# Three row tiles of the next block under way instead of two, in a streaming encoder layer on one core

## The chip, the cores and the metric

The kernel runs as one program on 1 core of one Trainium2 chip. The metric is the device time of one execution in microseconds (us); three executions of the kernel before are known, and their median is the time before. A profile of one further execution goes with them.

## The reference, cut to what matters

The reference is one layer of a streaming encoder over 2048 prompt rows and 64 sample rows of width 1024, in float32. What matters here is its first step, which every row goes through before the input projection:

```python
def rms_norm(x, g):
    xf = x.astype(jnp.float32)
    y = xf * lax.rsqrt(jnp.mean(xf * xf, axis=-1, keepdims=True) + NORM_EPS)
    return (y * g.astype(jnp.float32)).astype(x.dtype)

h = rms_norm(x, p['norm1_g']) * (1 + sc1) + sh1
z = h @ p['w_in']
```

`z` is then cut into a convolution branch, q, k and v of an attention over the row's own chunk of 64 and the 8 chunks before it, and two gates. Both branches are projected, gated and merged, projected again and added to the input; a feed-forward part with a second norm follows.

## The kernel before, in words

**Blocks and stages.** The 2112 rows (64 sample rows first) are worked in four blocks (`PBLOCKS`, line 35: 576 rows, then 512 three times) and then, from about 1200 us of the span, in three other blocks for merge, output projection and feed-forward. For each of the four blocks the stages run in the order of line 553: q, a quarter of the convolution's input, k, another quarter, v, the last two quarters, and the gates ("g"). Every product is made of three passes (`mm3`, line 700) of operands that are split in a high and a low part.

**The normed rows.** All products of a block read `hh` and `hl` (lines 1606, 1607): the normed, scaled and transposed rows of that block, high and low part, eight slices of 128 channels by up to 576 columns. There is one pair of them. So the rows of the next block are written into it while the gates of this block, its last readers, are still at work, columns first to last as they come free.

**One row tile.** `norm_tile` (line 1166) is a generator that prepares one tile of 128 rows of the next block, step by step; a `yield` ends a step and says when the next is due. Its steps are:

1. The row tile `x_t` is loaded (`load_ahead`, line 1160) into one of three buffers (tag "x", line 1164). Three tiles are loaded when the generators are made known; the fourth is loaded when the first tile has gone through its second group of transposes and left its buffer (line 1183).
2. The square (line 1147): ScalarE squares two halves of 512 with a running sum, into two scratch tiles `junk` of the ring "t" (seven buffers, line 773, which also holds the gates' results until their DMA has stored them, and others); VectorE adds the two sums and forms the mean; GpSimd raises it to the power -1/2 (`r`, line 740).
3. The scale (line 1175): VectorE multiplies the 128x1024 tile by `r`, in place.
4. Twice, for a group `g` of four slices: TensorE transposes four 128x128 pieces into a PSUM bank `pt` (line 1181), VectorE applies the norm's weight and shift into `h` (line 1187), the generator waits until the gates have left the columns it will write (line 1189), ScalarE writes `hh` (line 1191) and VectorE `hl` (line 1193).

**What orders the work.** The kernel is written as one stream of instructions around the matmuls. After a set of passes `stream.spend` (line 207) may make a tick, one per 500 ns of counted TensorE time, and at a tick each lane (`Lane`, line 108) may take one step of one of its generators. The lanes are the norm lane, q/k rows, attention heads, the convolution's tail and the convolution's taps (line 1604). The norm lane takes the first of its first `NORM_W` = 2 generators whose next step is due (line 146). So while the tiles with number 0 and 1 of the next block wait for columns, the tiles 2 and 3 are not begun; tile 2 is begun when tile 0 is done.

The norm lane gets the four generators of the next block when gate 11 of 16 is done (lines 1645 to 1650). The gates' last two pairs are worked in two halves of the columns, and `free["columns"]` is set after each half (line 1373). At stage q of the next block, `qkv` (line 1194) goes through the four tiles in order; for each it first steps the tile's generator to its end if it is not there yet (line 1210), and then writes the 24 matmuls of the product (line 1213). So the products of q meet the four tiles just after they were made. This happens three times in the kernel: at the ends of blocks 0, 1 and 2.

The framework that builds the program may put the instructions of one engine in another order than they were written in; each engine then works through its own list in that order. SyncE ("SP") issues nearly all DMAs, in one list too.

Of the kernel before, what the change touches and what calls it, by code (L numbers as in the profile page):

```python
# [16 lines left out]
P = 128  # L17
# [36 lines left out]
SIDE_G = 10  # L54
SPLIT_G = 2
NORM_G = 11
NORM_W = 2
SCORE_ROOM = {"dve": 2500}
TURN_NS = 600.0
POOL_BEHIND = 3000.0  # L60
# [4 lines left out]
def token_tiles(lo, hi):  # L65
    head = [(0, SMP)] if lo == 0 else []
    return head + [(t, P) for t in range(max(lo, SMP), hi, P)]
# [10 lines left out]
def tile_chunks(lo, hi):  # L78

    tiles = token_tiles(lo, hi)  # L80
    t, n = tiles[(len(tiles) + 1) // 2 - 1]
    return [(lo, t + n), (t + n, hi)]
# [529 lines left out]
def streaming_layer(ctx: ExitStack, tc: tile.TileContext, I, O):  # L612
# [87 lines left out]
    def mm3(ps, lh, ll, rh, rl, first, last, **kw):  # L700
        pe.matmul(ps, lh, rh, start=first, stop=False, **kw)
        pe.matmul(ps, lh, rl, start=False, stop=False, **kw)
        pe.matmul(ps, ll, rh, start=False, stop=last, **kw)
        stream.spend()
# [67 lines left out]
    def temp(name, shape=(P, 512)):  # L772
        return wk.tile(list(shape), F32, tag="t", name=name, bufs=NT)
# [312 lines left out]
    def v_rows(ps, n, t):  # L1086
        out = state_row(vs_p, vn_s, t, n)
        store_v(ps, n, kcol(t))
        if out is not None:
            v32 = temp("v32")  # L1090
            act.activation(v32[:n], ps[:n], AF.Copy)
            stream.at(stream.when("act"), lambda: nc.sync.dma_start(out, v32[:n]))
# [17 lines left out]
    def state_row(prompt, sample, t, n):  # L1110
        if t < SMP:
            return sample[:n]
        t -= SMP + SEQ - QB
        return prompt[t : t + n] if t >= 0 else None

    def kcol(t):
        return t + CACHE
# [16 lines left out]
    def load_mixed(c0, c1, i):  # L1134

        src = [[quarter("cin", i) for _ in range(2)] for _ in range(2)]
        for j, a in enumerate((c_d, o_d)):
            for l in range(2):
                nc.sync.dma_start(src[l][j][:, :, : c1 - c0].bitcast(F32), a[l, :, :, c0:c1].rearrange("c p t -> p c t"))
        return src  # L1140
# [6 lines left out]
    def square(x_t, n, junk=None):  # L1147
        ssq = wk.tile([P, 2], F32, tag="ssq", name="ssq", bufs=3)
        if junk is not None:
            act.activation(junk[:n], x_t[:n], AF.Square, accum_out=ssq[:n, 0:1])  # L1150
            return rsqrt_mean(wk, ssq[:n, 0:1], n, 1, D)
        for j in range(2):
            act.activation(temp("junk")[:n], x_t[:n, 512 * j : 512 * j + 512], AF.Square, accum_out=ssq[:n, j : j + 1])
        stream.after("dve", "act")
        dve.tensor_tensor(ssq[:n, 0:1], ssq[:n, 0:1], ssq[:n, 1:2], ALU.add)
        return rsqrt_mean(wk, ssq[:n, 0:1], n, 1, D)
# [3 lines left out]
    def load_ahead():  # L1160

        if to_load:
            t = to_load.pop(0)
            ahead_x[t] = load_x(t, P, wa, "x", 3), stream.load["pe"] + X_LAG

    def norm_tile(lo, t, free):

        c = slice(t - lo, t - lo + P)
        while t not in ahead_x:
            load_ahead()  # L1170
        x_t, landed = ahead_x.pop(t)
        yield landed
        r = square(x_t, P)
        yield stream.when("pool")
        dve.tensor_scalar(x_t, x_t, r, None, ALU.mult)
        yield stream.when("dve") + PE_LAG
        for g in range(2):
            pt = ps_g.tile([P, 4, P], F32, tag="gp", name="pt")
            h = temp("h32", (P, 4, P))
            for k in range(4):  # L1180
                pe.transpose(pt[:, k], x_t[:, (4 * g + k) * P : (4 * g + k + 1) * P], ident)
            if g:
                stream.at(stream.when("pe"), load_ahead, True)
            stream.after("dve", "pe")
            for k in range(4):
                kk = 4 * g + k
                dve.tensor_scalar(h[:, k], pt[:, k], A1[:, kk, 0:1], B1[:, kk, 0:1], ALU.mult, ALU.add)
            yield stream.when("dve")
            yield lambda: free["columns"] >= c.stop
            f = slice(4 * g, 4 * g + 4)  # L1190
            act.activation(hh[:, f, c], h, AF.Copy)
            yield stream.when("act")
            dve.tensor_tensor(hl[:, f, c], h, hh[:, f, c].bitcast(F32), ALU.subtract)
    def qkv(b, m, norms):
        lo, hi = PBLOCKS[b]
        tiles = token_tiles(lo, hi)
        ws = {}

        def product(t, n, ps, k):
            if k // 2 not in ws:  # L1200
                ws[k // 2] = W.get(("qkv", m, k // 2))
            wh, wl = ws[k // 2]
            c = slice(t - lo, t - lo + n)
            mm3(ps[:n], hh[:, k, c], hl[:, k, c], wh[:, k % 2], wl[:, k % 2], k == 0, k == KT - 1)
            if (t, n) == tiles[-1] and k % 2:
                W.done()

        for t, n in tiles:
            if t in norms:
                norm_lane.drain([norms[t]])  # L1210
            ps = ps_g.tile([P, 512], F32, tag="gp", name="ps")
            for k in range(KT):
                product(t, n, ps, k)
            if m == 0:
                work.start(qk_rows(ps, n, gqk[:, 0:1], q_d, t, None))
            elif m == 1:
                work.start(qk_rows(ps, n, gqk[:, 1:2], k_d, kcol(t), state_row(ks_p, kn_s, t, n), b == 0 and t > 2 * P))
            else:
                v_rows(ps, n, t)
# [244 lines left out]
    def attention(b):  # L1464

        heads = [(x, h) for h in range(NH) for x in ((0, "s") if b == 0 else (b,))]
        for head in heads:
            order.append(head)
            attn.add(attend(len(order) - 1))
# [130 lines left out]

    norm_lane, work = Lane({}, wide=NORM_W), Lane({}, wide=5)
    attn = Lane(ATTN, ATTN_NS, wide=2)
# [18 lines left out]
    for b, stage in ORDER:  # L1621
        lo, hi = PBLOCKS[b]
        if stage == "q":
            free, ahead = {"columns": 0}, {}
            if b + 1 < len(PBLOCKS):
                ahead = {t: norm_tile(hi, t, free) for t, _ in token_tiles(*PBLOCKS[b + 1])}
        if stage == "q" and b == 0:
            pass
        elif stage in ("q", "k", "v"):
            qkv(b, "qkv".index(stage), norms)  # L1630
            if stage == "k":
                work.wide = 3
            if stage == "v":

                def heads(b=b):
                    work.drain()
                    stream.flush()
                    attention(b)
                    if b == 3:
                        attn.burst, attn.spacing = 2, 0.0  # L1640

                stream.at(stream.load["pe"] + HEADS_NS, heads)
        elif stage == "g":
            for g in gates(b, free):
                if g == NORM_G:
                    to_load += list(ahead)
                    for _ in range(3):
                        load_ahead()
                    for gen in ahead.values():
                        norm_lane.add(gen)  # L1650
                if g == SIDE_G and b == len(PBLOCKS) - 1:
                    work.drain()
                    conv.drain()
                    stream.flush()
                    side.close()
                    wc = ctx.enter_context(tc.tile_pool(name="wc", bufs=1, side="right"))
                    cs = tile_chunks(*CBLOCKS[0])[0]
                    src = load_mixed(*cs, 0)
                    first_gates = gate_columns(*cs, 0)
            norms = ahead  # L1660
        else:
            if b == 0 and stage == 1:
                bias_rows()
            if stage == 0:
                conv.drain()
                tail.drain()
                y = wk.tile([P, 4, YW], F32, tag="y", name="y")
            conv.add(convolve(glu(b, stage), y, stage, b))
            if stage == 3:
                if b == 0:  # L1670
                    tail.add(conv_norm(y, 0, SMP, 0))
                    tail.add(conv_norm(y, SMP + HIST, QB, SMP))
                else:
                    tail.add(conv_norm(y, 0, QB, lo))
        for _ in range(MODS.get((b, stage), 0)):
            next(mods)
# [633 lines left out]
```

## Time and profile before

| what | value |
|---|---|
| time, median of three executions | 2967.82 us (2967.78 to 2973.06) |
| the profiled execution's own time | 2969.84 us |
| its span, first to last instruction | 2968.1 us |
| mean granted TensorE clock | 0.995 |
| TensorE busy | 2900.5 us |
| VectorE busy | 2024.0 us |
| ScalarE busy | 1357.8 us |
| GpSimd busy | 1129.0 us |

The rows of the trace name an engine (PE is TensorE, PEld its weight loads, DVE is VectorE, ACT is ScalarE, POOL is GpSimd, SPq is SyncE's DMA queue), the tile written, an arrow, the tiles read, and the shape. Nearly all carry line 102, that of a helper that records each operation, so rows are told apart by their tiles: `x_t`, `junk`, `ssq`, `t`, `r`, `pt`, `h`, `hh` and `hl` are the steps of `norm_tile`. A timeline row begins with the start and the duration in us; a bracket at its end, where there is one, gives the time for which the engine sat idle before it, and what ended that. Instructions of a kind that follow each other are merged into one row with their count.

### The profile page before, as it was taken

To read this page: it belongs to the slowest core of one execution; us is meant where nothing else is said; L and a number is where in the kernel's file an instruction comes from. 1 tells how busy PE (TensorE), PEld (TensorE's weight loads), DVE (VectorE), ACT (ScalarE), POOL (GpSimd) and SP (SyncE) were. 2 spreads that over 40 slices of the span, in tenths; PEclk is the share of its full clock that TensorE was granted. 3 is DMA by queue.
4 is the path that set the end of the run, shared out by engine and by line. 5 is a ranking of instruction groups with operands and counts; after the bars stand their busy time and mean duration, and the time that the engine had idled before them with its cause. 6 is when DMAs were issued, how large, how long until landed. Compare 5 with 4: busy or idle time off the path is not lost.

```text
span 2968.1 us, 44826 instructions
## 1 busy us (share of the span) xinstructions
PE 2900.5 (98%) x16199; PEld 2593.4 (87%) x16199; DVE 2024.0 (68%) x3632; ACT 1357.8 (46%) x2431; POOL 1129.0 (38%) x727
## 2 busy tenths in 40 slices
PE   7999899999999999989999999999999999999999
PEld 5899777887888788879999999999999999999998
DVE  5897687668857885577777746656666557466666
ACT  3345643661456257464443345434444345344442
POOL 1201310111011102444566452355666741465767
PEclk9999999999999999999999999999999999999999
DMA  9988889988997889885444786333333965333333
GB/s 319 307 281 294 267 291 309 282 260 275 302 285 220 281 252 283 274 280 173 146 154 148 251 260 229 113 100 96 114 121 110 322 231 184 96 94 113 114 105 126
DMA packets 467723, 628.05 MB, mean 212 GB/s; under 512 B 36276, under 2 KB 314664, under 8 KB 467501
## 3 DMA queue, kind: packets, MB, share of 16 engines
q1 hardware_dynamic: 453600, 606.11, 62.9%
q10 hardware_dynamic: 13901, 19.08, 1.9%
q8 instruction: 127, 2.08, 0.3%
q14 instruction: 95, 0.78, 0.1%
HBM read 476.53 MB, written 148.54 MB: 211 GB/s over the span
## 4 chain that ended last, share of the span: by engine, by line
PE 83%; DVE 7%; DMA 4%; ACT 2%; POOL 2%; issue 2%; SPq 0%; ACTq 0%; DVEq 0%; POOLq 0%
PE ps L102 54%; PE pd L102 16%; PE pw L102 6%; DVE y L102 2%; PE po L102 2%; PE sc L102 2%; PE ptp L102 2%; DVE wlo L102 1%; PE pt L102 1%; PE pa L102 1%; ACT whi L102 1%; DMA tg<-g_d 1%; POOL r L102 1%; DVE pw L102 1%; POOL wlo L102 0%
## 5 line engine op out<-in xcount | busy, mean ns | idle before, releaser
L102 PE MATMUL ps<-t,whi 128*128 128x384 f32 (+1 forms) x2112 | 502.8, 322 | 8.9 <-ACT t L102 4.9
L102 POOL TENSOR_TENSOR wlo<-wst,whi 128x1024 fp32r<-128x1024 f32 (+1 forms) x156 | 356.9, 2298 | 280.0 <-ACT whi L102 261.0
L102 ACT ACTIVATE whi<-wst 128x1024 fp32r<-128x1024 f32 (+1 forms) x263 | 256.8, 979 | 331.7 <-PE ps L102 125.1
L102 PE MATMUL ps<-b,whi 128*128 128x384 f32 (+1 forms) x1584 | 382.9, 327 | 6.9 <-DVE early L102 3.6
L102 PEld LDWEIGHTS ps<-t,whi 128*128 128x128 f32 x2112 | 367.7, 188 | 16.5 <-ACT t L102 5.1
L102 DVE SCALAR_TENSOR_TENSOR y<-u,wd,y 128x512 f32<-128x512 f32 (+1 forms) x480 | 369.2, 773 | 6.4
L102 PE MATMUL ps<-hh,whi 128*128 128x512 f32 (+2 forms) x992 | 362.1, 365 | 0.0
L102 DVE TENSOR_TENSOR acc<-acc,pd 128x512 f32<-128x512 f32 x464 | 311.8, 685 | 63.0 <-PE pd L102 60.4
L102 PE MATMUL ps<-hl,whi 128*128 128x512 f32 (+2 forms) x992 | 346.3, 349 | 0.0
L102 PE MATMUL ps<-hh,wlo 128*128 128x512 f32 (+2 forms) x992 | 345.8, 349 | 0.0
L102 PE MATMUL ps<-t,wlo 128*128 128x384 f32 (+1 forms) x1056 | 339.1, 321 | 0.7 <-POOL wlo L102 0.7
L102 PE MATMUL pd<-whi,hid 128*128 128x512 f32 x972 | 314.9, 390 | 0.3 <-DVE acc L102 0.3
L102 PEld LDWEIGHTS ps<-b,whi 128*128 128x128 f32 x1584 | 279.7, 190 | 12.8 <-DVE early L102 4.5
L102 PE MATMUL ps<-b,wlo 128*128 128x384 f32 (+1 forms) x792 | 257.6, 325 | 0.0
L102 POOL TENSOR_TENSOR r<-t,mhalf 128x1 f32<-128x1 f32 (+2 forms) x68 | 84.3, 1242 | 448.1 <-DVE t L102 436.9
L102 ACT ACTIVATE pr<-pr,sm 128x640 f32<-128x640 f32 (+3 forms) x272 | 200.1, 747 | 109.3 <-DVE sm L102 106.6
L102 PEld LDWEIGHTS pd<-whi,hid 128*128 128x128 f32 x972 | 182.4, 188 | 38.5 <-DVE acc L102 1.0
L102 PEld LDWEIGHTS ps<-hh,wlo 128*128 128x128 f32 x992 | 187.6, 189 | 21.6
L102 PEld LDWEIGHTS ps<-hh,whi 128*128 128x128 f32 x992 | 188.1, 190 | 18.4 <-issue 1.6
L102 PEld LDWEIGHTS ps<-hl,whi 128*128 128x128 f32 x992 | 188.3, 190 | 15.4 <-issue 1.4
L102 PEld LDWEIGHTS ps<-t,wlo 128*128 128x128 f32 x1056 | 198.1, 188 | 2.0 <-POOL wlo L102 1.3
L102 PE MATMUL pd<-wlo,hid 128*128 128x512 f32 x508 | 198.5, 391 | 0.0
(226 smaller groups left out, 6163.0 us busy)
## 6 DMA issues: line engine op xcount, KB each, us to landing
whi<-w_din_h SPq DMA_DIRECT2D x72, 512.0 KB, 6.6
wlo<-w_din_l SPq DMA_DIRECT2D x72, 512.0 KB, 7.0
wst<-sum_d SPq DMA_DIRECT2D x132, 256.0 KB, 3.1
wfo<-in_w_ffn_out SPq DMA_DIRECT2D x64, 512.0 KB, 3.4
wmod<-in_w_ada SPq DMA_DIRECT2D x46, 512.0 KB, 8.8
sum_d<-ws SPq DMA_DIRECT2D x88, 256.0 KB, 2.3
wst<-in_w_ffn_in SPq DMA_DIRECT2D x84, 256.0 KB, 3.2
wst<-in_w_in SPq DMA_DIRECT2D x40, 512.0 KB, 7.9
```

Of the source, the lines that this page charges most:

```text
L102: self.last = f(*args, **kw)
```

## The change

Three generators of the norm lane may be under way instead of two. The third and the fourth tile now stop before their transposes until the tile two places ahead of them has gone through all its steps: a counter `free["turned"]` is set by each tile at its end, and tile i (i > 1) waits for it to reach i - 1. Tile 2 can so be squared and scaled while tiles 0 and 1 wait for columns, and stands in its buffer until tile 0 is done. Loads, buffers and rings are as before.

```diff
-NORM_W = 2
+NORM_W = 3
...
         dve.tensor_scalar(x_t, x_t, r, None, ALU.mult)
         yield stream.when("dve") + PE_LAG
+        i = (t - lo) // P
+        if i > 1:
+            yield lambda: free["turned"] >= i - 1
         for g in range(2):
...
             dve.tensor_tensor(hl[:, f, c], h, hh[:, f, c].bitcast(F32), ALU.subtract)
+        free["turned"] = i + 1
...
-            free, ahead = {"columns": 0}, {}
+            free, ahead = {"columns": 0, "turned": 0}, {}
```

## The prediction

> **What bounds the kernel now.** I read the page's busy times first, then what TensorE waited for, then its timeline at the places where the next block's tiles are made. The busy row:
>
> ```profile
> PE 2900.5 (98%) x16199; PEld 2593.4 (87%) x16199; DVE 2024.0 (68%) x3632; ACT 1357.8 (46%) x2431; POOL 1129.0 (38%) x727
> ```
>
> TensorE is busy for 2900.5 of 2968.1 us, so the change can only pay through the time in which TensorE stands still because of a row tile. The head of the list of its waits (us in total, how often, the longest):
>
> ```profile
> PE pt L102 <- DVE x_t L102: 10.0, 5, 5.7
> PE sc L102 <- DVE sm L102: 5.7, 5, 2.4
> PE pm L102 <- POOL s L102: 5.6, 4, 1.9
> ```
>
> The largest entry of all is the one that the change touches: transposes (`pt`) that wait for a scaled tile (`x_t`), 10.0 us in five waits. The same list for 200 to 400 us alone begins:
>
> ```profile
> PE pt L102 <- DVE x_t L102: 9.5, 4, 5.7
> ```
>
> So 9.5 us of it lie there, at the end of block 0. The other two ends of a block lie near 600 and 900 us. A table of stretches (busy us with counts, granted clock, DMA share, GB/s):
>
> ```profile
> core 0: us, PE busy (x) PEld busy (x) DVE busy (x) ACT busy (x) POOL busy (x), PEclk, DMA share, GB/s
> ...
> 590.00:640.00 50.00, 50.00 (x322) 44.67 (x321) 34.49 (x88) 32.70 (x68) 3.87 (x5) 1.00 0.88 283
> 870.00:920.00 50.00, 49.51 (x317) 44.58 (x317) 33.85 (x86) 31.05 (x67) 4.25 (x5) 1.00 0.74 232
> ```
>
> There TensorE is busy for 50.00 and 49.51 of 50 us: nothing can be won, and I count these two ends at nothing. All of the gain must come from the first end. Its four waits on TensorE's timeline, with what stands around them:
>
> ```profile
> 301.31 0.66 PE L102 MATMUL pt<-ident,x_t 128*128 128x128 f32 x4 [1.89 <-DVE x_t L102]
> ...
> 305.81 0.33 PE L102 MATMUL pt<-ident,x_t 128*128 128x128 f32 x1 [0.64 <-DVE x_t L102]
> 306.01 0.50 PE L102 MATMUL sc<-kk,q 128*128 128x256 f32 x2
> ...
> 337.20 0.66 PE L102 MATMUL pt<-ident,x_t 128*128 128x128 f32 x4 [1.29 <-DVE x_t L102]
> ...
> 338.62 0.40 PE L102 MATMUL ps<-whi,hh 128*128 128x512 f32 x1
> 338.86 0.40 PE L102 MATMUL ps<-wlo,hh 128*128 128x512 f32 x1
> ...
> 349.17 1.09 PE L102 MATMUL pt<-ident,x_t 128*128 128x128 f32 x4 [5.65 <-DVE x_t L102]
> 350.37 0.79 PE L102 MATMUL ps<-whi,hh 128*128 128x512 f32 x1
> ```
>
> The first two waits (1.89 and 0.64 us) are those of tiles 0 and 1, whose steps the change leaves alone. The third, 1.29 us, is tile 2's, in the middle of tile 1's product. The fourth, 5.65 us, is at tile 3's transposes, which stand in the list ahead of tile 2's product; that begins at 350.37. One more thing is to be seen: the four transposes of which the first runs at 305.81 are one loop in the code, yet two score matmuls follow after one of them. So the order on an engine isn't the written one, and I can't read from the diff where tile 3's transposes will stand.
>
> **Why tiles 2 and 3 are late.** GpSimd and VectorE for tile 2:
>
> ```profile
> 331.23 4.63 POOL L102 TENSOR_TENSOR y<-y,s 128x512 f32<-128x512 f32 x4
> 335.81 0.56 POOL L102 TENSOR_TENSOR r<-t,mhalf 128x1 f32<-128x1 f32 x1
> ```
>
> ```profile
> 336.40 0.75 DVE L102 TENSOR_SCALAR x_t<-x_t,r 128x1024 f32<-128x1024 f32 x1 [4.92 <-POOL r L102]
> ...
> 347.05 0.16 DVE L102 TENSOR_TENSOR ssq<-ssq 128x1 f32<-128x1 f32 x1 [2.13 <-ACT junk L102]
> 347.13 0.40 DVE L102 TENSOR_SCALAR h<-pt,A,B 128x128 f32<-128x128 f32 x1
> ...
> 348.27 0.75 DVE L102 TENSOR_SCALAR x_t<-x_t,r 128x1024 f32<-128x1024 f32 x1 [0.23 <-POOL r L102]
> ```
>
> Tile 2's power sits on GpSimd behind four multiplications of the convolution's tail (4.63 us), and VectorE stands for 4.92 us at the tile's scale, with the scores' work behind it. The load and the square of tile 3, and tile 2's `hh`:
>
> ```profile
> 335.42 0.97 SPq L1144 DMA_DIRECT2D x_t<-in_x_prompt  x1
> ```
>
> ```profile
> 345.70 0.61 ACT L102 ACTIVATE junk<-x_t 128x512 f32<-128x512 f32 x1
> ...
> 349.69 0.63 ACT L102 ACTIVATE hh<-h 128x512 fp32r<-128x512 f32 x1 [0.61 <-DVE h L102]
> ```
>
> Tile 3 is loaded only at 335.42 and squared at 345.70. Tile 2's own `h` (347.13) stands on VectorE behind tile 3's sum (347.05), so its `hh` comes at 349.69, and at 350.37 tile 2's product begins with its operand just made: without tile 3's transposes ahead of it, it would have waited as long. The 5.65 us are charged to tile 3, but tile 2 is late too.
>
> **The change, part by part.** No instruction is added or removed; the square, power and scale of tile 2 move, and with them their places in the lists of ScalarE, GpSimd and VectorE. No DMA moves by itself: tile 3's load still hangs on tile 0.
>
> *Tile 2's norm moves forward*, by up to some 25 us, to just behind tile 1's. What it meets there, from tile 1's square on ScalarE:
>
> ```profile
> 301.83 0.63 ACT L102 ACTIVATE junk<-x_t 128x512 f32<-128x512 f32 x1 [2.44 <-DMA x_t<-in_x_prompt]
> ```
>
> On ScalarE it takes two halves of 0.63, 1.26 us, and perhaps a wait for the load like these 2.44 us; behind it stand the gates' tanh, which free TensorE's banks. I cost it at nothing: the 2.44 us held the same tanh back, and up to 306 us TensorE's only waits are for `x_t` itself (1.89 and 0.64). Without that cover it costs at most 2.44 + 1.26 = 3.7 us. The new wait for `turned` is a wait of the generator, not of an engine: nothing is queued behind it, and its transposes come when tile 0 is done, as before.
>
> *The 1.29 us at 337.20* go: the scale is done long before. VectorE's 4.92 us at the scale go too, so the scores' work behind it comes sooner.
>
> *The 5.65 us at 349.17.* TensorE comes to this point at 343.52 (349.17 less 5.65), now 1.29 us sooner, at 342.23. Tile 2's `hh` waits for nothing of tile 3 any more, so its 24 matmuls can run, at the 0.24 us from 338.62 to 338.86: 5.8 us, to 348.0. Next late is tile 3. If its square moves only with the scores ahead of it, by 1.29 us, its scale ends at 348.27 + 0.75 - 1.29 = 347.73; with 0.66 for the transposes, four `h` at 0.40 and 0.63 for `hh`, its product can begin at 350.6, a rest of 2.6 us. If the load holds the square at 345.70, the rest is 3.9 us. If 3 of the 4.92 us carry through to ScalarE, it is 0.9 us. I take 2.0, somewhat under the middle one, because some of the 4.92 us should carry. So 3.65 of 5.65 us go.
>
> *The clock after the rest.* The table of stretches again, and one from after the wait of 1.89 us:
>
> ```profile
> 343.50:347.00 3.50, 0.02 (x1) 0.00 (x0) 0.72 (x4) 3.22 (x10) 0.00 (x0) 1.00 1.05 336
> 347.00:349.20 2.20, 0.03 (x1) 0.07 (x2) 1.92 (x7) 2.03 (x5) 0.56 (x1) 0.60 1.03 407
> 349.20:352.00 2.80, 2.68 (x8) 1.88 (x9) 2.80 (x8) 0.63 (x1) 1.14 (x1) 0.50 1.07 233
> 352.00:355.00 3.00, 3.00 (x10) 2.34 (x9) 3.00 (x9) 2.98 (x6) 1.49 (x1) 0.62 0.45 126
> ```
>
> ```profile
> 301.30:304.00 2.70, 2.69 (x21) 2.69 (x22) 0.73 (x4) 1.76 (x6) 0.37 (x1) 1.00 0.34 87
> ```
>
> After 5.65 us of rest the granted clock (third number from the end) is 0.50 until 352 and 0.62 in the next 3 us. At most 0.50 of 2.68 us and 0.38 of 3.00 us are lost, 2.5 us; part of that time isn't paced by the clock, and I take 1.9. After the rest of 1.89 us the clock stayed at 1.00. With 2.0 us of rest left it should hold, so the 1.9 us go. The Trainium skill, "TensorE: Matmul & The Clock Gate", Part 1, says that an idle window of about 3.4 us halves the array's clock and that about 3.4 us of sustained work restore it. The trace agrees, with 1.00 in the first 3.5 us of the rest and 0.60 after them. By that rule the 1.9 us would not be won where the rest that is left outlasts the window, as in the case of the load.
>
> **The sum**: 1.29 + 3.65 + 1.9 = 6.8 us less. TensorE bounds what follows, at 98%, so it carries to the end. Against the profiled execution's own time that is 2969.84 - 6.8 = 2963.0 us; that execution stands 2.02 us above the median of 2967.82, so the forecast is **2961.0 us**. Its ends: at least 1.29 + (5.65 - 3.9) without the clock, 3.0 us (2964.8); at most 1.29 + (5.65 - 0.9) + 2.5, 8.5 us (2959.3).
>
> **The rivals.**
>
> *Tile 3's transposes keep their place ahead of tile 2's product.* For it: the builder put them there before. Against it: they filled a hole then, since tile 2's operand was late too. TensorE would rest until 347.73, and tile 2's product would follow the 0.66 us of transposes at 348.4 instead of 350.37: 2.0 us less, with as long a rest and so the same clock after it. 2965.8 us.
>
> *The early square isn't early.* Its two `junk` tiles need room in the ring of seven; if there is none until tile 0 is done, all stays as it is, 2967.8 us. Tile 1's two found room at 301.83 with tile 0's `h` parked, which speaks against it.
>
> *Slower: the ring blocks ScalarE.* The chain of work shows, just before the last part of tile 0's square, the store of a gate's result:
>
> ```profile
> 293.71 4.47 DMA g_d<-gate
> ```
>
> So the ring was full enough for a square to wait until a store had landed. With two more `junk`, a square or the next gate could stand in ScalarE's list for another store; the tanh behind it would free TensorE's banks late, and this at all three ends of a block, also where nothing is won. At 4.47 us each that is 13.4 us against 6.8 won: 6.6 us more, 2974.4 us. It decides from 2.3 us per end. Against it: the banks' slack, which covered the 2.44 us.
>
> **How the numbers follow.** Forecast 0.50, kept place 0.22, not early 0.08, ring 0.20. 0.2%, about what a measurement of this kernel can tell from no change, is 5.9 us. Of the forecast's 3.0 to 8.5 us, thickest at 6.8, I put seven parts in ten beyond it, 0.36, and add 0.02 from the kept place, for orders that also shorten other waits: faster 0.38. Of the ring's 0.20 I count 0.17 as slower, since it may hit one end alone. The rest, 0.45, is the same. The range goes from the forecast's best less 2 us, since the waits for `sm` and `s` above (5.7 and 5.6 us) may fall otherwise in a new order, 2957.3, to the ring's 2974.4.
>
> **What would show it.** Right: from 200 to 400 us TensorE's waits for `x_t` fall from 9.5 to about 4.5 us (1.89 + 0.64, and 2.0); tile 2's `junk` stands on ScalarE soon after 303 us; tile 2's product follows tile 1's without a rest; the clock stays at 1.00 through 355 us. Wrong: a rest of over 3.4 us ahead of tile 2's or tile 3's product; squares or `gate` rows on ScalarE with a wait for a store ahead of them; TensorE busy for less than 49 of the 50 us at the second or third end. A shift that arises behind 400 us, in work that the change doesn't touch, would show that the new order, and not the tiles, made the time.

## The result and the profile after

| | before | after |
|---|---|---|
| median | 2967.89 us (2961.99 to 2973.06, 20 runs) | 2972.61 us (2967.59 to 2978.36, 20 runs) |
| the profiled execution's own time | 2969.84 us | 2977.81 us |
| its span | 2968.1 us | 2976.0 us |

The ratio after to before is 1.0013, 95% interval [1.0007, 1.0019]: 4.7 us slower. That lies inside the 0.2% that the prediction took for no difference, but clear of 1. The prediction had said 6.8 us faster, so its sign was wrong.

The busy times on the page after (us, share, instructions):

```profile
PE 2901.3 (97%) x16199; PEld 2592.0 (87%) x16199; DVE 2026.4 (68%) x3632; ACT 1356.7 (46%) x2431; POOL 1127.3 (38%) x727
```

TensorE has the same work (2901.3 us against 2900.5), and the mean granted clock is 0.995 in both profiles. So the longer span is rest. What TensorE waited for between 200 and 400 us (the two entries that matter here; us in total, times, longest):

```profile
PE pt L102 <- DVE x_t L102: 8.1, 3, 5.2
PE sc L102 <- DVE sm L102: 3.0, 1, 3.0
```

The wait for row tiles fell from 9.5 us in four waits to 8.1 in three. One wait went, the 1.29 us at tile 2. The long one stayed, and a wait of 3.0 us at the scores (`sc`) is new: 11.1 us in place of 9.5. (The step of VectorE that writes `sm`, a number per row for the softmax, reads a PSUM bank of scores; after it TensorE may write the next scores there.) The sum of 8.1 us alone would show nothing: a second profile of the kernel before (before_again, below) has 8.1 us in three waits as well, since the first two waits differ from execution to execution. But tile 2's wait stands in it, with 1.23 us.

**What went as meant.** ScalarE after squares tile 2 (the second pair) right behind tile 1 (the first):

```profile
300.44 0.63 ACT L102 ACTIVATE junk<-x_t 128x512 f32<-128x512 f32 x1 [3.39 <-DMA x_t<-in_x_prompt]
...
301.07 0.61 ACT L102 ACTIVATE junk<-x_t 128x512 f32<-128x512 f32 x1
...
301.98 0.62 ACT L102 ACTIVATE junk<-x_t 128x512 f32<-128x512 f32 x1
...
302.74 0.62 ACT L102 ACTIVATE junk<-x_t 128x512 f32<-128x512 f32 x1
```

**The new wait.** VectorE after, at tile 2's scale, and GpSimd at the same time (`wlo` is the low part of a split weight, made by a subtraction):

```profile
305.28 2.82 DVE L102 TENSOR_SCALAR x_t<-x_t,r 128x1024 f32<-128x1024 f32 x1 [0.66 <-POOL r L102]
308.02 0.28 DVE L102 CUSTOM_DVE_ANT_0 pr<-sc,bias 128x128 f32<-128x128 f32 x1
```

```profile
304.69 0.55 POOL L102 TENSOR_TENSOR r<-t,mhalf 128x1 f32<-128x1 f32 x1 [1.89 <-DVE t L102]
305.21 2.34 POOL L102 TENSOR_TENSOR wlo<-wst,whi 128x1024 fp32r<-128x1024 f32 x1
```

The scale takes 2.82 us instead of 0.75. It begins 0.07 us after a subtraction of GpSimd and ends 0.55 us after it. In the kernel before, the same two meet the other way round at tile 1; first GpSimd, then VectorE:

```profile
305.15 2.84 POOL L102 TENSOR_TENSOR wlo<-wst,whi 128x1024 fp32r<-128x1024 f32 x1 [0.96 <-ACT whi L102]
```

```profile
305.00 0.75 DVE L102 TENSOR_SCALAR x_t<-x_t,r 128x1024 f32<-128x1024 f32 x1
```

There VectorE came first by 0.15 us, and GpSimd's subtraction took 2.84 us instead of 2.34. The change puts a third scale into this place, and this one comes second. That is no chance of one execution: the scale waits for the power `r`, and the subtraction stands next to that power in GpSimd's own list, so both begin when it ends, GpSimd 0.07 us ahead. The scale takes 2.82 to 2.86 us in all nine profiles of kernels that make tile 2's scale early on VectorE and have the attention in its place. The Trainium skill, "SBUF — State Buffer", section "Who interferes with whom", calls the port pair that the two engines share an exclusive lock: whoever issues first has it for the whole instruction, and the other blocks fully. The rows of the two scales and the two subtractions agree, in both orders.

Behind the long scale the score's own step on VectorE (308.02) is late, and TensorE waits for it. TensorE's timeline after, there and at tile 3:

```profile
308.36 0.80 PE L102 MATMUL sc<-kk,q 128*128 128x256 f32 x2 [3.02 <-DVE sm L102]
...
349.23 1.11 PE L102 MATMUL pt<-ident,x_t 128*128 128x128 f32 x4 [5.25 <-DVE x_t L102]
349.99 0.78 PE L102 MATMUL ps<-whi,hh 128*128 128x512 f32 x1
```

**The kept wait.** Tile 3's transposes stand where they stood, ahead of tile 2's product, though that product's operand was now ready long before. They wait 5.25 us, and the product begins at 349.99 (350.37 before; counted from a common row, see the ruler below, it is no earlier). Tile 3 itself is no earlier: SyncE issues its load at 339.21 (335.42 before), ScalarE squares it at 345.89:

```profile
339.21 0.93 SPq L1144 DMA_DIRECT2D x_t<-in_x_prompt  x1
```

```profile
345.89 0.61 ACT L102 ACTIVATE junk<-x_t 128x512 f32<-128x512 f32 x1
```

Stretches of the kernel after (busy us with counts of PE, PEld, DVE, ACT and POOL; then granted clock, DMA share, GB/s), and the same of before:

```profile
304.00:308.40 4.40, 0.96 (x7) 0.73 (x7) 3.70 (x7) 0.75 (x3) 2.85 (x2) 0.99 0.99 291
308.40:312.00 3.60, 3.60 (x10) 2.57 (x11) 1.90 (x8) 1.33 (x5) 0.00 (x0) 0.54 1.02 407
...
349.90:352.00 2.10, 2.10 (x8) 1.72 (x7) 2.10 (x7) 1.01 (x2) 1.61 (x1) 0.50 1.04 413
352.00:355.00 3.00, 3.00 (x18) 2.35 (x17) 2.73 (x6) 2.42 (x5) 0.46 (x1) 0.89 1.07 283
590.00:640.00 50.00, 50.00 (x320) 45.02 (x319) 31.85 (x79) 32.27 (x69) 1.67 (x3) 1.00 0.87 283
640.00:690.00 50.00, 47.82 (x280) 38.94 (x279) 33.23 (x69) 23.56 (x43) 7.30 (x6) 1.00 0.76 238
```

```profile
304.00:308.40 4.40, 3.77 (x23) 2.81 (x22) 3.80 (x15) 2.87 (x9) 3.03 (x2) 1.00 0.65 162
308.40:312.00 3.60, 3.60 (x27) 3.51 (x26) 3.41 (x11) 3.35 (x8) 1.45 (x1) 1.00 1.04 410
...
640.00:690.00 50.00, 49.72 (x289) 41.36 (x288) 32.49 (x64) 22.41 (x40) 7.49 (x5) 1.00 0.78 249
```

The first two rows, against those of before, are the price of the new wait: 2.8 us less work by 308.4, and then 10 matmul records in place of 27 at a clock of 0.54 instead of 1.00. The last row is a second place: from 640 to 690 us TensorE works 47.82 instead of 49.72 us. The stretch from 590 to 640 us, on which the prediction judged the end of block 1, is full in both.

**A ruler.** Executions differ from each other by some 5 us, much of it before the first tile of block 1. So I measure stages inside one profile, between rows that every kernel has: the first score row behind 284 us (`sc<-kk`, at 289.74 before and 288.08 after), and the last copy of a block's values on ScalarE (`vst`) for blocks 1, 2 and 3. The copies of blocks 1 and 2 before, then after:

```profile
456.02 0.60 ACT L102 ACTIVATE vst<-ps 128x512 fp32r<-128x512 f32 x1 [4.89 <-PE ps L102]
...
739.55 0.60 ACT L102 ACTIVATE vst<-ps 128x512 fp32r<-128x512 f32 x1 [4.84 <-PE ps L102]
```

```profile
458.76 0.60 ACT L102 ACTIVATE vst<-ps 128x512 fp32r<-128x512 f32 x1 [4.89 <-PE ps L102]
...
745.09 0.60 ACT L102 ACTIVATE vst<-ps 128x512 fp32r<-128x512 f32 x1 [4.84 <-PE ps L102]
```

So the stage of the first end takes 456.02 - 289.74 = 166.3 us before and 458.76 - 288.08 = 170.7 after; that of the second, 739.55 - 456.02 = 283.5 and 286.3. By this ruler tile 3 is later after than before: its load is issued 5.45 us later, its scale begins 1.8 us later, and tile 2's product 1.3 us later.

The profiles by this ruler (us), with the ratio of the times. The last three runs leave out part of block 1's convolution and are compared with each other. The late runs of the experiments are not in it: their first score row behind 284 us stands near 399 us.

| kernel (name of the run) | first end | second end | third end | time, ratio to before |
|---|---|---|---|---|
| before | 166.3 | 283.5 | 276.3 | |
| before, once more (before_again) | 165.9 | 283.9 | 278.2 | 1.0001 [0.9992, 1.0011] |
| after | 170.7 | 286.3 | 278.1 | 1.0013 [1.0007, 1.0019] |
| after, once more (again) | 168.5 | 285.5 | 277.3 | 1.0008 [0.9999, 1.0017] |
| change at the first end only (first_end) | 167.5 | 283.1 | 278.8 | 1.0013 [1.0004, 1.0023] |
| at the later ends only (later_ends) | 167.8 | 288.8 | 275.8 | 1.0003 [0.9995, 1.0012] |
| the scale on ScalarE (act_scale) | 160.4 | 292.0 | 280.7 | 1.0014 [1.0005, 1.0022] |
| tile 3 held back (hold_t3) | 171.4 | 288.2 | 275.7 | 1.0021 [1.0012, 1.0030] |
| ceiling (same_x) | 168.3 | 292.5 | 276.3 | 1.0013 [1.0004, 1.0022] |
| only the new wait (yield_only) | 166.4 | 284.1 | 279.7 | 1.0012 [1.0003, 1.0021] |
| only the width (width_only) | 165.0 | 284.2 | 278.7 | 1.0015 [1.0002, 1.0028] |
| wait at the first end only (wait_first) | 170.4 | 283.6 | 277.7 | 1.0003 [0.9994, 1.0013] |
| another constant, PE_LAG (order_a) | 165.9 | 291.4 | 274.5 | 1.0030 [1.0019, 1.0042] |
| another constant, ATTN_NS (order_b) | 166.7 | 298.8 | 278.1 | 1.0076 [1.0064, 1.0089] |
| before, fewer taps (half_before) | 165.6 | 282.0 | 275.0 | 0.9996 [0.9987, 1.0005] |
| after, fewer taps (half_after) | 169.8 | 284.0 | 275.8 | 1.0022 [1.0012, 1.0033] |
| ceiling, fewer taps (half_same_x) | 172.1 | 284.6 | 276.9 | 1.0013 [1.0004, 1.0022] |

Nearly the same work lies between the rows in each: in act_scale six matmuls of the attention stand behind the first end instead of ahead of it, and in order_b the first row comes 12 matmuls later in TensorE's list.

The two profiles of before agree within 0.4 us at the first two ends and differ by 1.9 us at the third. Other kernels whose lists are the same over a stage lie further apart: after, again, first_end and wait_first at the first end from 167.5 to 170.7, after, again, later_ends and hold_t3 at the second from 285.5 to 288.8. So I compare groups: the first end with the changed list (167.5 to 170.7) and the second with the changed list (285.5 and more) don't overlap with before (165.9 to 166.3, with order_a, whose list there is that of before, and 283.5 to 283.9). At the first end the distance is small: yield_only and later_ends have one and the same list there, without the change of width, and stand at 166.4 and 167.8. So less than some 1.5 us tells nothing at that end. A ratio has an interval of about 0.09% to each side, 2.7 us: it tells the large differences only.

### The profile page after: what moved, and what is told of

It is laid out like the page before. It is cut to its first block, busy times and chain, and to the rows that moved or that the text cites. A ratio compares the mean times of both kernels' runs of the same rounds, so it can differ in the third digit from the quotient of the medians.

```text
span 2976.0 us, 44837 instructions
## 1 busy us (share of the span) xinstructions
PE 2901.3 (97%) x16199; PEld 2592.0 (87%) x16199; DVE 2026.4 (68%) x3632; ACT 1356.7 (46%) x2431; POOL 1127.3 (38%) x727
## 4 chain that ended last, share of the span: by engine, by line
PE 79%; DVE 9%; DMA 6%; ACT 2%; issue 2%; POOL 2%; SPq 0%; ACTq 0%; POOLq 0%; DVEq 0%
PE ps L102 51%; PE pd L102 15%; PE pw L102 5%; DVE y L102 3%; PE sc L102 2%; PE po L102 2%; PE ptp L102 2%; DVE wlo L102 1%; DMA tg<-g_d 1%; PE pt L102 1%; POOL r L102 1%; PE pa L102 1%; DVE pw L102 1%; ACT whi L102 1%; DMA wmod<-in_w_ada 1%
## 5 line engine op out<-in xcount | busy, mean ns | idle before, releaser
L102 PEld LDWEIGHTS ps<-hl,whi 128*128 128x128 f32 x992 | 188.6, 190 | 15.7 <-issue 1.4
```

Of the source, the lines that this page charges most:

```text
L102: self.last = f(*args, **kw)
```

## The experiments

### Which end, and is it the collision?

**again**: the changed kernel itself.

> The changed kernel once more, to see which places of its loss come back. Theory 1 (collision at the first end: tile 2's early scale on VectorE runs into a wlo subtraction of GpSimd and takes 2.82 us instead of 0.75): 2972.6 us, and the 2.8 us scale, the wait of about 3 us ahead of the scores' matmuls near 308 us and the granted clock near 0.54 behind it come back in the new profile. Theory 2 (the attention's order is laid differently behind 400 us, and TensorE's waits there make the time): 2972.6 us, with the small waits near 416, 422 and 650 us back at the same places. Theory 3 (the profile caught chance): both sets of waits are gone or elsewhere, and the time is within 0.2% of the kernel before.

The collision came back: the scale takes 2.82 us again, TensorE waits 3.0 us, and the small waits near 416, 422 and 650 us stand at their places. The ratio of 1.0008 takes in 1 and the first ratio.

**first_end** and **later_ends**: in the loop that adds the generators, the lane's width is set by block (`b > 0` in place of `b == 0` in later_ends):

```diff
                 if g == NORM_G:
+                    norm_lane.wide = 3 if b == 0 else 2
```

> Three tiles under way at the end of block 0 only. Theory 1 (collision at the first end): about 2972 us, some 4 us over the kernel before, all of the loss. Theory 2a (order laid differently at the ends of blocks 1 and 2): 2967 to 2968 us, no loss, or a gain of up to 2 us. Theory 2b (order of the attention between 400 and 440 us, which hangs on the first end): about 2971 us, and its waits are behind 400 us.

> Three tiles under way at the ends of blocks 1 and 2 only. Theory 1 (collision at the first end) and theory 2b (attention between 400 and 440 us): 2967 to 2968 us, as before. Theory 2a (order laid differently at these two ends): about 2971 to 2972 us, with waits of TensorE near 650 and 906 us that the kernel before does not have.

By the times the first end alone loses as much as the whole change, and the later ends alone lose nothing that shows. By the ruler the first end alone loses 1.2 to 1.6 us there and nothing at the second; the later ends alone lose 4.9 to 5.2 us at the second end. The two measures weigh the ends differently, and neither end is free. In first_end the list up to the second end is that of the changed kernel, the scale collides again (2.86 us), but TensorE came later to the score and waited 1.0 us instead of 3.0: its first end, 167.5 us, is the shortest of the four with this list (170.7, 168.5, 170.4). Up to the first input tanh of block 1 (`tb` on ScalarE, at 373.41 us after) first_end takes 82.4 us from the ruler's first row and the other three 84.5 to 85.3, so the wait costs some 2 to 3 us by these four.

That place isn't where most of the first end's loss arises, though. Up to `tb` the list of before needs 82.8 to 83.7 us in three profiles (with order_a), with some six matmuls fewer done by then. From `tb` to the stage's end the four with the changed list need 83.8 to 85.9 us, the three others 82.6 to 83.1, though now the changed list has the six matmuls less to do. So the larger part lies behind 373 us, where TensorE's waits for the attention near 415 and 422 us are other ones than before.

**act_scale**: the width as in first_end, and tile 2's scale at the end of block 0 on ScalarE:

```diff
-        dve.tensor_scalar(x_t, x_t, r, None, ALU.mult)
...
+        if i == 2 and lo == 576:
+            stream.after("act", "pool")
+            act.activation(x_t, x_t, AF.Copy, scale=r)
...
+        else:
+            dve.tensor_scalar(x_t, x_t, r, None, ALU.mult)
```

> Three tiles under way at the end of block 0 only, and tile 2's scale there done by ScalarE (about 1.1 us) instead of VectorE, so that it can't meet GpSimd's wlo on VectorE. Theory 1 (collision): the wait of about 3 us at 308 us and the half clock behind it go, and against the variant with the first end alone some 4 us come back: about 2966 to 2968 us. Theories 2a and 2b (order of the attention): the same time as the variant with the first end alone, within 1.5 us.

The collision is gone, and the stretch at 308 us is full at full clock. The time isn't better. Its stretches, with 500 to 560 us, where the kernel before works 57.99 us:

```profile
304.00:308.40 4.40, 4.40 (x28) 3.65 (x27) 4.16 (x15) 4.12 (x11) 2.18 (x1) 1.00 0.92 328
308.40:312.00 3.60, 3.60 (x30) 3.60 (x29) 1.48 (x4) 3.60 (x7) 2.26 (x1) 1.00 1.04 403
500.00:560.00 60.00, 54.55 (x268) 44.61 (x267) 45.82 (x81) 29.83 (x51) 7.08 (x8) 0.94 0.79 258
```

The first end is 5.6 to 5.9 us shorter than before, and the second 8.1 to 8.4 us longer. There TensorE waits once for 4.59 us at the attention's scores, and the clock is 0.50 in the 3 us from there:

```profile
539.03 1.43 PE L102 MATMUL sc<-kk,q 128*128 128x320 f32 x4 [4.59 <-DVE sm L102]
```

The collision was the cause of the new wait, but taking it away brings the time nowhere. As this edit lays the later order anew too, it doesn't price the collision by itself.

### Is it tile 3's kept place?

**hold_t3**: tile 3's transposes at the end of block 0 wait until 18 of the 24 matmuls of tile 2's product are written.

```diff
+        if i == 3 and lo == 576:
+            yield lambda: "begun" in mid
         for g in range(2):
...
                 product(t, n, ps, k)
+                if (b, m, t - lo, k) == (1, 0, 2 * P, 5):
+                    mid["begun"] = True
```

> The changed kernel, but tile 3's transposes at the end of block 0 are held back until tile 2's product is three quarters done. Theory K (they keep their place ahead of tile 2's product, and that keeps the 5.25 us of rest and its half clock): the rest ahead of them falls to 2 to 3 us, tile 2's product follows tile 1's with no rest, and the time falls by 3 to 5 us against the changed kernel, to 2967.5 to 2969.5 us. Theory O (the attention's chain paces this stretch, so a rest that is taken away comes back at the scores): the rest goes too, but TensorE's waits for sm, pr or pl between 350 and 620 us grow by as much, and the time stays at 2971 to 2973 us.

**same_x**, the ceiling:

```diff
+        if i == 3 and lo == 576:
+            x_t = mid["x"]
+        else:
             r = square(x_t, P)
...
+        if i == 2:
+            mid["x"] = x_t
```

> A ceiling: at the end of block 0 tile 3 takes tile 2's scaled rows (its own square, power and scale are left out, its load is still made), so nothing of tile 3 can be late. Theory K (tile 3's lateness and kept place cost the rest): all 5.25 us of rest and its half clock go, 5 to 7 us against the changed kernel: 2965.5 to 2967.5 us. Theory O (the attention's chain paces this stretch): at least half of that comes back as waits for sm, pr or pl by 620 us: 2969 to 2972 us.

Both took the 5.25 us ahead of tile 2's product away; both keep the collision, with its 3.0 us. What TensorE waited for between 280 and 520 us, in hold_t3, in same_x, and in the kernel before:

```profile
PE sc L102 <- DVE sm L102: 6.4, 5, 3.0
PE pt L102 <- DVE x_t L102: 2.7, 2, 1.5
PE ps L102 <- ACT hh L102: 2.2, 1, 2.2
PE ptp L102 <- ACT pr L102: 1.3, 2, 0.7
```

```profile
PE sc L102 <- DVE sm L102: 6.4, 6, 3.0
PE sc L102 <- DMA kk<-k_d: 3.2, 1, 3.2
PE ptp L102 <- ACT pr L102: 2.2, 4, 0.9
PE pt L102 <- DVE x_t L102: 2.1, 2, 1.2
```

```profile
PE pt L102 <- DVE x_t L102: 9.5, 4, 5.7
PE sc L102 <- DVE sm L102: 4.4, 3, 2.4
```

The waits for tiles (`x_t`, `hh`) go from 9.5 us (8.1 in the kernel after) to 4.9 and 2.1. The attention's (`sm`, `pr`, and `kk`, keys read back from memory) are 7.7 and 11.8 us, against 4.4 before and 8.2 in the kernel after; the collision's 3.0 us are in all but the 4.4. So against the kernel after they grow in same_x alone: the times are those of theory O, but its mechanism shows in one of the two. In hold_t3 it is smaller waits that fill the place: from 350 to 359 us TensorE waits four times, 4.3 us in all, and the clock behind them is 0.50 (358.4 to 361 us). With the smaller entries, the sums are 15.5 and 15.7 us, against 14.4 before and 16.6 in the kernel after. In same_x the first input tanh of block 1 (`tb`) comes 76.9 us behind the ruler's first row, against 83.7 before: 6.8 us won. At the end of the stage it is 2.0 us behind, and at that of the next 11.1 us, with the 3.2 us wait for `kk` in it. This ceiling was there to show that the predicted 6.8 us can be had. Here they are won, and lost again within some 90 us. Theory K fell: the kept place is real, but removing it gains nothing in the time.

With the attention in its place no run takes both the collision and tile 3's lateness away. act_scale comes nearest: it has no collision, and its waits around tile 3 are 0.34 us for `x_t` and 2.96 us for `hh`. It is ahead to the end of the stage, and gives that back at 539 us.

### Which part of the change?

**yield_only** (`NORM_W = 2` in the changed kernel) and **width_only** (the two lines of the wait left out).

> Two tiles under way as before, with only the new wait of the generator for the first tile's turn, which is always fulfilled and can only shift the order of the instructions. Theory K and the collision theory: nothing is early and nothing is held, so 2967 to 2968.5 us. Theory R (any re-laid order of the attention around the ends of a block costs some us): 2969.5 to 2971 us, with about 2 us of it at the end of block 2, where the variant with the first end alone lost 2.3 us with this same order.

> Three tiles under way, without the wait for the first tile's turn: the third tile's transposes may be issued at once. Theory K: tile 2's own matmuls were on time with the wait as well, tile 3 is as late as before, so the time is that of the changed kernel, 2971 to 2974 us. Theory W (the wait costs: it holds tile 2's transposes back): 2 to 4 us less than the changed kernel, 2968 to 2970 us.

The ruler finds nothing at the first two ends in yield_only (+0.1 to +0.5 and +0.2 to +0.6 us) and a gain of 0.9 to 1.3 us at the first end in width_only; the times give both 3.6 and 4.5 us more, with intervals that begin at 0.9 and 0.6 us. Where those come from, a single profile doesn't show; part may lie at the third end, which is 0.5 to 3.4 us longer in the two than in the two profiles of before. Theory W finds no support in the times. But by the ruler the loss of the kernel after at the second end needs wait and width together; at the first end it looks the same, within the scatter (later_ends, with the wait alone there, stands at 167.8).

**wait_first** keeps the width of three everywhere, and the wait at the end of block 0 only:

```diff
-        if i > 1:
+        if i > 1 and lo == 576:
             yield lambda: free["turned"] >= i - 1
```

> The changed kernel, with the wait for the first tile's turn at the end of block 0 only. If the wait makes the loss of 2.3 us at the end of block 1 (all four profiles with wait and width there show it, the one without the wait doesn't): the stage from 597 to 690 us loses less than 0.5 us, TensorE's waits for sm and pl near 650 to 667 us go, and the time is 2 us below the changed kernel, near 2970 us. If the width makes it: the stage loses 2.3 us as before.

TensorE's waits from 597 to 690 us, after and in wait_first:

```profile
PE sc L102 <- DVE sm L102: 1.3, 1, 1.3
PE pt L102 <- DVE pl L102: 0.4, 1, 0.4
PE po L102 <- DVE pl L102: 0.3, 1, 0.3
```

```profile
PE sc L102 <- DMA kk<-k_d: 0.3, 1, 0.3
```

The second end is back at 283.6 us, and in all five profiles with width and wait there it is 285.5 to 292.5. So the loss of 1.6 us or more at the end of block 1 needs the wait there, beside the width. That it works through the places that tiles 2 and 3, and with them the attention's steps, get in the list fits the waits that come and go, but is argued, not shown. The ratio is 1.0003.

### Does VectorE's load, or the attention, take the gain back?

**half_before**, **half_after**, **half_same_x**: block 1's convolution with fewer taps, in the kernel before, the changed kernel and the ceiling.

```diff
-        for k in range(1, TAPS):
+        for k in range(1, 16 if b == 1 else TAPS):
```

> The kernel before with 15 of the 30 taps of block 1's convolution left out (4 x 15 x 0.75 us = 45 us of VectorE's work between 375 and 550 us). Theory V (VectorE's load paces the attention in this stretch): TensorE's waits for sm and pr between 400 and 500 us (2.40, 0.92, 1.04) shrink to under 2 us in all, and the time falls by 3 to 5 us. Theory L (the steps of the attention wait for each other, whatever else VectorE does): the waits stay, time within 2 us of the kernel before.

> The changed kernel with the same 15 of 30 taps of block 1 left out. Theory V: its waits between 400 and 500 us (1.39, 1.15, 0.61, 0.41, 0.93, 1.03) shrink to under 2 us, and it comes to within 1.5 us of the kernel before with half the taps, or below it. Theory L: they stay, and it stays 3 to 5 us above the kernel before with half the taps.

> The ceiling (at the end of block 0 tile 3 takes tile 2's scaled rows, so nothing of tile 3 is late) with the same 15 of 30 taps left out. Theory V: what the missing rest wins (7.6 us by 373 us) is kept, and it ends 4 to 7 us below the kernel before with half the taps. Theory L: it is given back by 500 us as waits for sm, pr, pl or kk, and it ends within 2 us of that kernel or above it.

The ratios are 0.9996 [0.9987, 1.0005], 1.0022 [1.0012, 1.0033] and 1.0013 [1.0004, 1.0022]. So the change loses here too, in a pair of kernels of its own, and the ruler finds 4.2 us of it at the first end and 2.0 at the second. The head of the waits of half_same_x between 280 and 520 us:

```profile
PE sc L102 <- DVE sm L102: 11.5, 7, 4.7
PE pt L102 <- DVE x_t L102: 1.8, 2, 1.3
```

With 60 tap steps less on VectorE (its busy time is 1982.3 us in half_before and 2024.0 in the kernel before) the wait for `sm` is larger than the 6.4 us of same_x, not smaller. Theory V fell: VectorE's load isn't what takes the gain back.

**late_before**, **late_after**, **late_same_x**: block 0's attention is added with block 1's, so the stretch from 300 to 390 us holds none.

```diff
-                    attention(b)
+                    if b == 1:
+                        attention(0)
+                    if b:
+                        attention(b)
```

> The kernel before with block 0's attention moved behind block 1's values, so that no score, transpose of weights or product of the attention lies in the list between 300 and 450 us. No theory speaks of its time against the kernel before; it is the base for the next two.

> The changed kernel with block 0's attention moved in the same way. Theory L (what TensorE wins at the tiles it gives back at the attention's own steps): with no attention there, nothing is given back: it ends 2 to 7 us below the kernel before with the late attention. Theory D (what is won is given back anyway, for instance at the weights' loads, or any new order costs some us): it ends 2 to 5 us above it.

> The ceiling (tile 3 takes tile 2's scaled rows at the end of block 0) with the late attention. Theory L: the rest of the tiles goes and stays away: 6 to 12 us below the kernel before with the late attention. Theory D: within 2 us of it, or above.

The ratios are 1.0043 [1.0030, 1.0056], 1.0061 [1.0047, 1.0075] and 1.0056 [1.0043, 1.0068]. Without the attention there is hardly a rest for tiles to begin with. All of TensorE's waits from 280 to 400 us in late_before, then in late_same_x:

```profile
PE ps L102 <- DVE hl L102: 2.4, 1, 2.4
PE pt L102 <- DVE x_t L102: 1.6, 1, 1.6
```

```profile
PE pt L102 <- DVE kn L102: 2.5, 1, 2.5
PE ps L102 <- DMA whi<-w_din_h: 0.7, 1, 0.7
```

The 4.0 us for tiles go, and 2.5 us of them come back at once at the k rows' norm (`kn`). In late_after, in the same window, small waits of at most 1.5 us make 4.4 us. From block 0's last `vst` copy to block 1's the three take 235.9, 235.4 and 234.5 us, though in late_after and late_same_x no scale is longer than 0.76 us at this end and in late_before one takes 2.91. So theory L holds only in a wider form: it need not be the attention; the next chain that feeds TensorE is late in the tiles' place. The medians of the two lie 5 to 7 us behind late_before's, though the intervals of the ratios overlap. In the profiles that arises late: at block 3's last `vst` copy both are some 10 us ahead (969.57 and 969.92 against 979.58), with 52 more matmuls of the attention still to do. From 1010 to 1220 us, where the attention that was put off is worked, TensorE waits 14.2 us in late_before, 20.7 in late_after, 19.4 in late_same_x. That part is the order of the attention again, and it is on theory D's side, though no wait for weights above 0.8 us shows in it.

### How much does an order cost by itself?

**before_again** is the control without any edit. **order_a** (`PE_LAG` 450 for 400) and **order_b** (`ATTN_NS` 650 for 600) change one constant each by which the planner places steps.

> The kernel before itself, run as if it were a variant. It shows how far a ratio can lie from 1 with nothing changed, and what one profile differs from the next in the same stage. All theories: 1.000 within 0.001, and stages that shift by no more than 2 us against the first profile. A ratio of 1.0012 would make the losses of the other variants chance.

> The kernel before, with one constant of the planner changed (PE_LAG 450 instead of 400): no tile is earlier and nothing is held, only the order of the instructions differs, in about as many places as by the change. Theory R (a newly laid order costs some us by itself, since the one before happens to fit well): 2 to 5 us over the kernel before, as every variant so far. Against it: within 2 us of it, or below.

> The same with another constant (ATTN_NS 650 instead of 600), which re-lays the attention in all blocks. Theory R: 2 to 10 us over the kernel before. Against it: within 2 us of it, or below.

The control gives 1.0001. The two constants cost 0.30% (8.9 us) and 0.76% (22.6 us), by the ruler 7.5 and 14.9 us of it at the second end, against the higher profile of before. No tile is early in them and no wait is added. Theory R holds for these two: re-laying the order costs as much as, and more than, the change was thought to win. That no variant with all the reference's work was clearly faster than the kernel before fits: it seems to sit at a favourable order. That rests on two constants, each moved one way only. It isn't shown that every other order is worse; wait_first and later_ends can't be told from it.

## Why the prediction was wrong

- *Tile 2's norm moves forward, at nothing*: it moved, and it wasn't free. The cover named was the banks' slack against ScalarE's 1.26 us. The price came on VectorE: 2.82 us in place of 0.75 beside GpSimd, 3.02 us of rest, and a clock of 0.54 behind it. The rows for it stood in the profile before (GpSimd 2.84 us at 305.15), but I had asked only what the square meets, not what the scale meets.
- *The 1.29 us at 337.20 go*: right.
- *3.65 of the 5.65 us at 349.17 go*: wrong, 0.40 went. The first rival, that tile 3's transposes keep their place, is what happened, and its 2.0 us less did not come either, since tile 3's scale stayed where it was (348.42 after, 348.27 before), its load being 3.8 us later.
- *The clock after the rest, 1.9 us*: mostly wrong. The rest outlasted 3.4 us, as the prediction's own sign for it said, and the clock fell to 0.50 again; it was back sooner (0.89 from 352 to 355 us, 0.62 before). That much was luck: wait_first has the same list for TensorE there, and 0.73 in the stretch at the same distance behind the rest (347.2 to 350.2 us).
- *"TensorE bounds what follows, at 98%, so it carries to the end"*: **the step that failed, even with all the others granted.** same_x removed the whole rest at tile 3 and had won 6.8 us at the first tanh; at the end of the stage it was 2.0 us behind. act_scale was 5.6 to 5.9 us ahead at the end of the stage and 2.5 to 2.6 behind at the end of the next. 98% is a mean over the kernel. In this stretch several chains feed TensorE, and when the tiles' was early in same_x and late_same_x, the scores, the keys or the k rows were late in its place.
- *The second and third ends at nothing*: wrong at the second, by 1.6 to 2.8 us. The stretch that I judged by, 590 to 640 us, is full before and after; the loss lies at 640 to 690 us, behind it. At the third end the kernel after shows no more than chance (278.1 and 277.3, against 276.3 and 278.2).
- *The ring blocks ScalarE* (the slower rival): not seen; ScalarE squares tile 2 without waiting for a store. The sign was the rival's, the mechanism not.
- The sign given for "the new order, and not the tiles, made the time", a shift that arises behind 400 us in work that the change doesn't touch, did appear: at 415 to 424 us and at 640 to 690 us.

What adds up: 2.2 to 4.8 us at the first end (after and again against both profiles of before), 1.6 to 2.8 at the second; the times say 2.1 to 5.6 us for the whole, by the ratio's interval. Still open is the 3.6 and 4.5 us of yield_only and width_only, which their profiles don't show, and why just this order fits: that other orders cost time is shown for two of them, and not explained.

## What to carry to other kernels

Where several chains feed one busy engine, a rest of that engine isn't worth its length: make a ceiling kernel that removes the late operand outright, and measure what is left at the end of the stage before arguing about how to remove it. When an edit goes through a planner that lays out all the work, run one or two controls that change the order and nothing else: if those move the time by more than the edit is worth, the edit's own mechanism can't be read from the time. And price a moved instruction on its own engine at its new place, port neighbours included, not only the engine that does the longest part of it.

## What the runs showed of the hardware

A scale of VectorE from SBUF to SBUF (128x1024, 0.75 us) and a subtraction of GpSimd (128x1024, 2.34 us) did not run side by side where they met: the one that came second was longer by about the other's remaining time (2.82 and 2.84 us). In before_again, where the scale ended (302.03 us) before the subtraction began (302.48), they took 0.74 and 2.40 us.

The clock fell after less than 3.4 us of rest: to 0.54 after 3.02 us at 308.36, and in first_end to 0.72 (301.5 to 304.9 us) after 2.23 us. After the 1.89 us of the kernel before it had stayed at 1.00. And once it fell after no long rest at all. In the kernel after, TensorE works 2.24 of the 4 us from 420 us, with waits of 1.15 and 0.61 us; then the same kernel once more, at the same place:

```profile
420.00:424.00 4.00, 2.24 (x15) 1.39 (x13) 3.96 (x12) 3.48 (x9) 0.00 (x0) 1.00 1.01 398
424.00:428.00 4.00, 4.00 (x13) 3.18 (x12) 4.00 (x9) 1.32 (x5) 0.00 (x0) 0.57 1.07 386
```

```profile
420.00:424.00 4.00, 2.23 (x12) 1.49 (x12) 3.96 (x11) 3.58 (x11) 0.00 (x0) 1.00 1.02 389
424.00:428.00 4.00, 4.00 (x23) 3.27 (x22) 3.96 (x9) 1.07 (x4) 0.00 (x0) 1.00 0.99 367
```

TensorE's work, its order and the rests are the same, and the clock is 0.57 in one and 1.00 in the other. At 0.57, 4 us are worth 1.7 us less; the first ends of the two differ by 2.2 us. So what a rest costs in clock is partly chance, and this is one source of the scatter. The Trainium skill, "TensorE: Matmul & The Clock Gate", Part 1, says that the gate watches a free-running window. The two pairs of rows agree with that; its about 3.4 us of idleness is not the bound that they show.

On ScalarE the same scale took 1.14 us beside such a subtraction, which at 2.38 us was no longer than the others (2.39 to 2.42). And executions of one unchanged kernel scatter by some 5 us each way, and much of that is there by the first score row: it stands at 284.5 us in wait_first and at 289.6 in first_end, whose lists for TensorE are the same up to there. Stages measured inside a profile repeat better: to 0.4 us at two ends of three in the kernel before, to 2.2, 0.8 and 0.8 us in the kernel after.
